# Gate sums moved to the seam, output-gate blocks over five banks, and a sink column, in a hybrid attention block

## The chip, the cores and the metric

The kernel runs on one core of a Trainium2 chip. Its time is the device time of one execution in microseconds (us); the figure of a kernel is the median of several runs. Five engines work side by side and wait for one another by semaphores: PE (matrix products), DVE and POOL (elementwise work), ACT (functions of one argument, copies and casts), and SP, which here only issues DMA transfers. An engine carries out its own instructions strictly in the order in which they stand in its queue.

## The reference

The reference is one decoder layer over 1024 positions of width 1024. All of it is computed in float32.

```python
mod = c @ w_ada[l] + b_ada[l]
shift, scale, gate = jnp.split(mod, 3, axis=-1)
h = rms_norm(x, g_pre[l]) * (1.0 + scale[:, None, :]) + shift[:, None, :]
proj = h @ w_in[l]
q_a, kv_c, kv_s, kv_w, g_nsa, z_a, q_b, kv_b, z_b, merge = jnp.split(proj, pts, axis=-1)
kc = compress_blocks(...)                       # an MLP over overlapping blocks of keys; vc alike
o_a = gts[0] * o_cmp + gts[1] * o_slc + gts[2] * o_win    # compressed, selected, window attention
y_a = (merge_heads(o_a) * jax.nn.silu(z_a)) @ w_o_nsa[l]
o_b = banded_attention(qb, kb, vb, slopes_b, SWA_WINDOW, sinks=sinks[l])
y_b = (merge_heads(o_b) * jax.nn.silu(z_b)) @ w_o_swa[l]
m_a, m_b = jnp.split(merge, 2, axis=-1)
y = (jax.nn.sigmoid(m_a) * y_a + jax.nn.sigmoid(m_b) * y_b) @ w_out[l]
x = x + gate[:, None, :] * rms_norm(y, g_post[l])
```

Two places matter below. The eight 128-row parts of `gate` are needed only by the last line. And the sliding-window attention (`o_b`) has one sink per head, a score that takes part in the softmax's sum and has no value behind it.

## The kernel before

Every float32 product is made of three passes of a matmul over a high and a low part: a weight tile `wraw` is loaded, its high part `wh` is a cast (rounded), and the low part `wl` is the difference, made on POOL (L177). The activations `h` stand in SBUF as `hh` and `hl` in two halves of 512 columns. The three matmuls are L200, L207, L208 in the early blocks, L998, L1003, L1004 in the later ones, L1361 to L1363 in the last part. The sums go to PSUM, whose eight banks are three pools by name: `b_s` (3), `b_pt` (2), `b_pv` (1), `b_pj` (2).

In order of time the kernel does this:

- A prologue (to about 95 us): the norm, the shift and scale, the first projections.
- The z stage (about 95 to 184 us). Six output-gate blocks (ZB0 to ZB3, ZA0, ZA1), each in two halves, are projected into a bank `b_pj`; ACT takes tanh of it (L562), DVE makes the gate (L563) in the tile `sp`, and SP stores that to DRAM (L564). `sp` has one buffer. Between them lie two MLPs that compress keys and values: their first weights come in 16 tiles `w1raw`, cast on ACT (L642), subtracted on DVE (L643), and multiplied on PE (L646 to L648); then come `he` (L650 to L653) and the rest. Beside it POOL makes four input combinations T1 to T4 in eight-way pieces (L731 to L738), which SP stores (L740); DVE makes the gate sums: for each of eight row blocks two products with a reduction over 512 columns (L723), on `w_ada` rows loaded into `wraw`'s buffers. The casts to `wh` in this stage are on DVE (L171), later ones on ACT (L174).
- Units B0 and B1 (184 to about 303 us): sliding-window attention of two key groups. In a task, scores (L856, L859) get the distance added and a running minimum on DVE (L866), exp on ACT (L878), and the sink is added by a subtraction (L884), an exp (L885) and an addition (L886) before the reciprocal (L887).
- Unit A0 (303 to 503 us) and unit A1 (503 to 709 us): the three attentions of the other mixer, one key group each. Between their steps stands a "line" of projection parts that a planner spreads evenly over the unit's PE columns; transfers and casts are hung ahead of a part or behind it. In unit A0 the line holds keys, queries, the blocks ZA2 and ZA3, and the first products of a Strassen-like scheme. In unit A1 it holds products on the sums T2, T1, T3, T4: a set is loaded from DRAM by `set_load` into the place of a half of `h` that is done with (L1049), and formed by `set_form` (cast on ACT, L1056, subtraction on POOL, L1057). Weight sums for the scheme (`paced_sums`, L700 to L706 on POOL) are put at fixed shares of unit A0.
- The seam (709 to 731 us): eight `seam_part`s of 12 matmuls each finish four merge gates; DVE adds their parts (L1345, L1346, L1349), and the heads 4 to 7 of mixer B are loaded (L1311) and split (cast on ACT L1312, subtraction on DVE L1313).
- The gated products of mixer B and then of mixer A (to about 817 us) and the final product (to the end). Beside them DVE and POOL make combinations of the rows of `w_out` (L1411, L1416, and others).

A scheduler orders each engine's queue by the order of the code and by priorities; ties that cost no semaphore ("pace") hold an instruction behind another one in that order.

## Time and profile before

| what | us |
|---|---|
| median of 3 runs | 902.82 (902.55 to 903.59) |
| the profiled execution | 906.57 |
| its span, first to last instruction | 904.7 |
| PE busy in it | 872.4 (96%) |
| DVE / ACT / POOL busy | 659.8 / 530.0 / 537.4 |

The span is the stretch that the trace shows; 1.87 us of the profiled execution lie outside it, and the profiled execution itself is 3.75 us above the median. Mean granted TensorE clock over the span is 0.986 of full speed.

### The profile page before, as it was taken

What the parts mean: (1) busy time and instruction counts of PE and PEld (TensorE: products, weight loads), DVE (VectorE), ACT (ScalarE), POOL (GpSimd) and SP (SyncE); (2) the same over time, 40 slices, a digit from 0 to 9 for tenths busy, and PEclk for the clock granted to TensorE, in tenths of its full rate; (3) what the DMA queues carried; (4) which work ended last, traced back from release to release, by engine and by line L of the source; (5) the groups of instructions that cost most, each with busy time, mean ns of one, the idle gap of its engine ahead of it and who ended that gap; (6) DMA issues with size and microseconds to landing.
All of it is one profiled execution on the core that took longest, in us unless ns stands there. A gap on an engine that the chain in (4) does not pass through costs nothing.

```text
span 904.7 us, 14788 instructions
## 1 busy us (share of the span) xinstructions
PE 872.4 (96%) x4418; PEld 731.0 (81%) x4418; DVE 659.8 (73%) x1637; ACT 530.0 (59%) x1200; POOL 537.4 (59%) x547
## 2 busy tenths in 40 slices
PE   8999988999999989999999999999999999999996
PEld 6989767788888768888888787888888788887885
DVE  4866887648878668666766587776677299788996
ACT  6466631156777777666657697665656375444331
POOL 1001987168786699676446788555666369735551
PEclk8999998999999999999999999999999999999998
DMA  9876566666455456342132533333253399841323
GB/s 352 276 273 206 197 210 223 219 216 208 135 172 156 151 190 185 117 162 72 42 100 72 188 109 120 114 122 124 105 199 128 105 346 303 299 128 59 105 93 117
DMA packets 93297, 151.46 MB, mean 167 GB/s; under 512 B 10913, under 2 KB 28705, under 8 KB 93218
## 3 DMA queue, kind: packets, MB, share of 16 engines
q1 hardware_dynamic: 92064, 149.30, 49.8%
q10 hardware_dynamic: 1154, 1.23, 0.5%
q8 instruction: 35, 0.57, 0.2%
q14 instruction: 44, 0.36, 0.1%
HBM read 108.81 MB, written 38.01 MB: 162 GB/s over the span
## 4 chain that ended last, share of the span: by engine, by line
PE 74%; DMA 3%; DVE 3%; issue 1%; ACT 1%; POOL 0%; DVEq 0%; POOLq 0%; SPq 0%; ACTq 0%
PE b_pt L927 8%; PE b_pj L998 7%; PE b_pj L1003 6%; PE b_pj L1004 6%; PE b_s L859 4%; PE b_pv L938 4%; PE b_s L856 4%; PE b_pv L935 4%; PE b_pj L200 3%; PE b_pj L207 3%; PE b_pj L208 3%; PE b_s L1363 1%; PE b_s L1361 1%; PE b_s L1362 1%; DMA wraw<-in_w_adaT 1%
## 5 line engine op out<-in xcount | busy, mean ns | idle before, releaser
L177 POOL TENSOR_TENSOR wl<-wraw,wh 128x512 fp32r<-128x512 f32 x123 | 170.0, 1386 | 98.8 <-ACT wh L174 80.9
L934 DVE TENSOR_TENSOR pl<-b_pt,ph 128x512 fp32r<-128x512 f32 x162 | 110.6, 686 | 47.4 <-ACT ph L933 46.5
L933 ACT CAST ph<-b_pt 128x512 fp32r<-128x512 f32 x162 | 93.2, 584 | 59.9 <-PE b_pt L927 50.8
L878 ACT ACTIVATE ps<-ps,mins 128x256 f32<-128x256 f32 (+7 forms) x128 | 81.2, 635 | 33.8 <-DVE mins L866 32.9
L174 ACT CAST wh<-wraw 128x512 fp32r<-128x512 f32 x115 | 70.6, 617 | 42.6 <-PE b_pj L1003 18.7
L856 PE MATMUL b_s<-kh,q 128*128 128x256 f32 (+6 forms) x272 | 86.2, 323 | 3.9 <-DVE mins L866 3.0
L200 PE MATMUL b_pj<-hh,wh 128*128 128x512 f32 x208 | 83.7, 403 | 5.2 <-DVE sp L563 5.2
L859 PE MATMUL b_s<-kl,q 128*128 128x256 f32 (+6 forms) x272 | 83.5, 314 | 0.0
L207 PE MATMUL b_pj<-hl,wh 128*128 128x512 f32 x208 | 83.3, 400 | 0.0
L208 PE MATMUL b_pj<-hh,wl 128*128 128x512 f32 x208 | 83.0, 400 | 0.0
L890 POOL TENSOR_SCALAR ps<-ps,rr,gates 128x128 f32<-128x128 f32 (+7 forms) x64 | 52.4, 822 | 50.9 <-DVE rr L882 42.2
L998 PE MATMUL b_pj<-hh,wh 128*128 128x512 f32 x188 | 78.3, 416 | 0.0
L1003 PE MATMUL b_pj<-hl,wh 128*128 128x512 f32 x188 | 74.7, 397 | 0.0
L1004 PE MATMUL b_pj<-hh,wl 128*128 128x512 f32 x188 | 74.4, 396 | 0.0
L938 PE MATMUL b_pv<-pl,V 128*128 128x512 f32 x162 | 68.4, 422 | 1.4 <-DVE pl L934 1.3
L935 PE MATMUL b_pv<-ph,V 128*128 128x512 f32 x162 | 66.6, 411 | 2.7 <-ACT ph L933 1.5
L927 PE MATMUL b_pt<-ident,ps 128*128 128x128 f32 x408 | 67.3, 274 | 0.4 <-DVE pl L934 0.4
L856 PEld LDWEIGHTS b_s<-kh,q 128*128 128x128 f32 x272 | 51.2, 188 | 13.5 <-DVE mins L866 5.2
L890 POOL TENSOR_SCALAR pw<-pw,rr,gates 128x640 f32<-128x640 f32 (+4 forms) x64 | 47.4, 742 | 22.4 <-DVE rr L882 19.6
L927 PEld LDWEIGHTS b_pt<-ident,ps 128*128 128x128 f32 x408 | 51.3, 141 | 10.7 <-DVE pl L934 0.8
L859 PEld LDWEIGHTS b_s<-kl,q 128*128 128x128 f32 x272 | 51.2, 189 | 7.2
L878 ACT ACTIVATE pw<-pw,mins 128x640 f32<-128x640 f32 (+4 forms) x64 | 44.5, 695 | 18.2 <-DVE mins L866 18.0
(454 smaller groups left out, 2474.2 us busy)
## 6 DMA issues: line engine op xcount, KB each, us to landing
wraw<-in_w_blk SPq DMA_DIRECT2D x83, 256.0 KB, 2.9
r<-in_w_out SPq DMA_DIRECT2D x32, 256.0 KB, 4.8
wa<-in_w_adaT SPq DMA_DIRECT2D x15, 512.0 KB, 5.1
wraw<-sS SPq DMA_DIRECT2D x28, 256.0 KB, 2.8
...
```

The lines of the kernel that those rows point to most:

```text
L177: chain("wl", nc.gpsimd.tensor_tensor(wl, raw, wh.bitcast(F32), ALU.subtract))
L200: ins = nc.tensor.matmul(t, lhsT=wh, rhs=hh[kc][half], start=(kc == 0), stop=False)
L207: nc.tensor.matmul(t, lhsT=wh, rhs=hl[kc][half], start=False, stop=False)
L208: nc.tensor.matmul(t, lhsT=wl, rhs=hh[kc][half], start=False, stop=(kc == KC - 1))
L856: ins = nc.tensor.matmul(sp[:, :n_in], lhsT=q, rhs=rh, start=True, stop=False)
L859: nc.tensor.matmul(sp[:, :n_in], lhsT=q, rhs=rl, start=False, stop=True)
L878: nc.scalar.activation(rows[r][:, :off], rows[r][:, :off], AF.Exp, scale=-1.0, bias=last_min[:, r : r + 1], accum_out=sums[:, r : r + 1])
L927: ins = nc.tensor.transpose(t[:, r * P : r * P + P], rows[r][:, off : off + P], ident)
L934: nc.vector.tensor_tensor(pl, t, ph.bitcast(F32), ALU.subtract)
L998: ins = nc.tensor.matmul(self.t, lhsT=wh[:, kc, :], rhs=hi, start=(self.first is None and kc == 0), stop=False)
L1003: nc.tensor.matmul(self.t, lhsT=wh[:, kc, :], rhs=lo, start=False, stop=False)
L1004: ins = nc.tensor.matmul(self.t, lhsT=wl[:, kc, :], rhs=hi, start=False, stop=(kc == KH - 1 and self.stop))
```

## The change

Six things change. The gate sums leave the z stage and are made at the seam, in eight full-width pieces of 1024 columns. The output-gate blocks use `b_s` and `b_pj` by turns, and their tile `sp` has three places: two of three go to the pool `kt` (six buffers). Ten of the twelve `wh` casts of the z stage go from DVE to ACT. The input sums T1 to T4 are tied, in the schedule, to the starts of the output-gate halves (`z_marks`). The sink is written as a 257th column of the score row, so that the one exp with its sum covers it. In unit A0 the output-gate blocks stand last in the line, the T2 and T1 sets are loaded four parts earlier and the first two pieces of T2 formed there, and the weight sums come later; in unit A1 forms are spread one by one.

```diff
     def split_half(raw, shape, low=None):
@@
         if low is None and hold[0] is None and not ended:
-            ins = nc.vector.tensor_copy(wh, raw)
-            after(ins, last["dve"])
+            cast_count[0] += 1
+            if cast_count[0] < 3:
+                after(ins := nc.vector.tensor_copy(wh, raw), last["dve"])
+            else:
+                after(ins := nc.scalar.copy(wh, raw), last["act"])
@@
-        z_out(name, half, proj_half(w, half, lambda: bank("pj")))
+        z_out(name, half, proj_half(w, half, lambda: bank(("s", "pj")[z_count[0] % 2])))
@@
-        sp = kq.tile([P, HS], F32, name="sp", tag="sp", bufs=1)
+        z_count[0] += 1
+        if hold[0] is None and z_count[0] % 3:
+            sp = kq.tile([P, HS], F32, name="sp", tag="kt", bufs=6)
+        else:
+            sp = kq.tile([P, HS], F32, name="sp", tag="sp", bufs=1)
@@
-    for k in range(8):
-        gate_sum(k)
-    nc.vector.tensor_tensor(amod, mod[:, 16:24], g_post, ALU.mult)
@@
-                    row = whole_row[:, 256 * r : 256 * r + 256]
+                    if r == 0:
+                        sink = 128 * min(i, 1) + 128
+                        nc.scalar.copy(whole_row.rearrange("p (r c) -> p r c", r=4)[:, :, sink],
+                                       nsink[:, 4 * g : 4 * g + 4])
+                    row = whole_row[:, 257 * r : 257 * r + 257]
@@
-            nc.vector.tensor_tensor(rr, last_min, nsink[:, 4 * g : 4 * g + 4], ALU.subtract)
-            nc.scalar.activation(rr, rr, AF.Exp)
-            nc.vector.tensor_tensor(sums, sums, rr, ALU.add)
@@
-                line += raw_products([2, 3]) + plan_z("A", 2) + raw_products([4]) + plan_z("A", 3)
-                line += plan_k(1, 0) + plan_q("A", 1, 0) + raw_products([5, 6])
+                line += raw_products([2, 3, 4]) + plan_k(1, 0) + plan_q("A", 1, 0) + raw_products([5, 6])
+                za, zb = plan_z("A", 2), plan_z("A", 3)
+                line += za[:2] + zb[:2] + za[2:] + zb[2:]
@@
-                behind(line[-1], half_free)
+                behind(line[-5], half_free)
+                for k in range(2):
+                    ahead_of(line[k - 2], lambda k=k: set_form("T2", (k,)))
@@
-                    for f, share in zip(paced_sums(p), (0.02, 0.07)):
-                        pieces.append((begun + whole[u] * (share + 0.14 * n), lambda at, f=f: f()))
+                    for f, share in zip(paced_sums(p), (0.18, 0.23)):
+                        paced(share + 0.09 * n, f)
@@
+        gate_c = op.tile([P, S], F32, name="cg", tag="oh0")
+        places = ["oh1", "oh2", "oh3", "ol0", "ol1"]
+        def gate_load(k):
+            wa = op.tile([P, S], F32, name="wg", tag=places[k % 5])
+            nc.sync.dma_start(wa, io["w_adaT"][(16 + k) * P : (17 + k) * P, :])
+            owing.append((16 + k, wa))
+        def gate_sum():
+            blk, wa = owing.pop(0)
+            nc.vector.tensor_tensor_reduce(
+                out=wa, in0=wa, in1=gate_c, scale=1.0, scalar=smalls[:, 8 + blk : 9 + blk],
+                op0=ALU.mult, op1=ALU.add, accum_out=mod[:, blk : blk + 1])
```

At the seam the transfer of `c` and two `gate_load`s stand in each of the four rounds behind the loads of that round, and two `gate_sum`s in each round but the first; the last two follow the loop.

The first place is DVE's queue in the z stage, from the fourth low part of the first MLP's weights on. `w1` are these weights, `wh` are casts, `he` is the MLP's hidden tile, `gpart` a half gate sum, `sp` the output gates. Before:

```order
L643 TENSOR_TENSOR w1_1195<-w1raw_1192,w1_1194 128x512
L643 TENSOR_TENSOR w1_1207<-w1raw_1204,w1_1206 128x512
L635 TENSOR_TENSOR fl_1176<-flat_1168,fh_1175 128x2048
L171 CAST wh_1591<-wraw_1587 128x512
L643 TENSOR_TENSOR w1_1219<-w1raw_1216,w1_1218 128x512
L651 TENSOR_SCALAR he_1146<-he_1146 126x256
L171 CAST wh_1595<-wraw_1589 128x512
L652 RECIPROCAL he_1146<-he_1146 126x256
L563 SCALAR_TENSOR_TENSOR sp_1441<-sp_1441,b_pj_1416 128x512
L653 TENSOR_TENSOR he_1146<-b_pt_1049,he_1146 126x256
L723 ISA wraw_1799,gpart_1730<-wraw_1799,cg_1731,smalls_79 128x512
L723 ISA gpart_1730 128x1
```

After:

```order
L654 TENSOR_TENSOR w1_1195<-w1raw_1192,w1_1194 128x512
L654 TENSOR_TENSOR w1_1207<-w1raw_1204,w1_1206 128x512
L646 TENSOR_TENSOR fl_1176<-flat_1168,fh_1175 128x2048
L654 TENSOR_TENSOR w1_1219<-w1raw_1216,w1_1218 128x512
L662 TENSOR_SCALAR he_1146<-he_1146 126x256
L663 RECIPROCAL he_1146<-he_1146 126x256
L574 SCALAR_TENSOR_TENSOR sp_1441<-sp_1441,b_pj_1416 128x512
L664 TENSOR_TENSOR he_1146<-b_pt_1049,he_1146 126x256
L574 SCALAR_TENSOR_TENSOR sp_1483<-sp_1483,b_s_1457 128x512
L669 COPY h1T_1154<-b_pt_1151 128x252
L574 SCALAR_TENSOR_TENSOR sp_1512<-sp_1512,b_pj_1487 128x512
```

The casts and the half sums are gone from DVE's queue between the MLP's steps, and the blocks' `sp` come from `b_s` and `b_pj` by turns.

The second place is the seam, from the last merge gates on. On DVE, `t2` are the merge gates, `wg` the gate sums, `r` rows of `w_out`, `ol7` the low part of the last head of mixer B, which the gated products need. Before:

```order
L1346 TENSOR_TENSOR t2_8789<-t2_8789,b_pt_8798 128x512
L1313 TENSOR_TENSOR ol6_8677<-t1_8678,oh6_8676 128x512
L1349 TENSOR_TENSOR t2_8789<-t2_8789,b_s_8820 128x512
L1345 TENSOR_TENSOR t2_8835<-t2_8835,b_pj_8845 128x512
L1313 TENSOR_TENSOR ol6_8677<-t1_8682,oh6_8676 128x512
L1346 TENSOR_TENSOR t2_8836<-t2_8836,b_pj_8845 128x512
L1411 TENSOR_TENSOR r_8919<-r_8919,r_8918 128x512
L1349 TENSOR_TENSOR t2_8836<-t2_8836,b_s_8867 128x512
L1416 TENSOR_TENSOR r_8922<-r_8923,r_8919 128x512
L1411 TENSOR_TENSOR r_9023<-r_9023,r_9022 128x512
L1313 TENSOR_TENSOR ol7_8687<-t1_8688,oh7_8686 128x512
L1313 TENSOR_TENSOR ol7_8687<-t1_8692,oh7_8686 128x512
```

After:

```order
L1359 ISA wg_8718,mod_83<-wg_8718,cg_8610,smalls_79 128x1024
L1359 ISA mod_83 128x1
L1378 TENSOR_TENSOR t2_8767<-t2_8767,b_pj_8781 128x512
L1379 TENSOR_TENSOR t2_8768<-t2_8768,b_pj_8781 128x512
L1359 ISA wg_8720,mod_83<-wg_8720,cg_8610,smalls_79 128x1024
L1359 ISA mod_83 128x1
L1384 TENSOR_TENSOR t2_8768<-t2_8768,b_s_8804 128x512
L1451 TENSOR_TENSOR r_8860<-r_8860,r_8859 128x512
L1359 ISA wg_8771,mod_83<-wg_8771,cg_8610,smalls_79 128x1024
L1359 ISA mod_83 128x1
L1327 TENSOR_TENSOR ol7_8601<-t1_8602,oh7_8600 128x512
L1327 TENSOR_TENSOR ol7_8601<-t1_8606,oh7_8600 128x512
```

Seven gate sums stand before the two `ol7` instructions now (four of them further up), and two of the three operations on `r` stand behind them. On SP, in the same place, `od7` is that head, `w_o` the weights of the gated products, the first of which here belongs to the fourth block. Before:

```order
L1389 DMA r_8923<-in_w_out 128x512
L1389 DMA r_9022<-in_w_out 128x512
L1389 DMA r_9023<-in_w_out 128x512
L1389 DMA r_9026<-in_w_out 128x512
L1311 DMA t1_8688<-od7_125 128x512
L164 DMA wraw_9039<-in_w_o 128x512
L1311 DMA t1_8692<-od7_125 128x512
L164 DMA wraw_9092<-in_w_o 128x512
L164 DMA wraw_9149<-in_w_o 128x512
```

After:

```order
L1354 DMA wg_8720<-in_w_adaT 128x1024
L1429 DMA r_8859<-in_w_out 128x512
L1429 DMA r_8860<-in_w_out 128x512
L1354 DMA wg_8771<-in_w_adaT 128x1024
L1325 DMA t1_8602<-od7_125 128x512
L1429 DMA r_8863<-in_w_out 128x512
L1325 DMA t1_8606<-od7_125 128x512
L1429 DMA r_8864<-in_w_out 128x512
L1429 DMA r_8963<-in_w_out 128x512
L1325 DMA t1_8912<-od0_118 128x512
L1429 DMA r_8964<-in_w_out 128x512
L1429 DMA r_8967<-in_w_out 128x512
L164 DMA wraw_8980<-in_w_o 128x512
L164 DMA wraw_9033<-in_w_o 128x512
```

From the first load of the seam (`od4`) up to that `w_o`, 23 transfers of 256 KB were asked for before (5.75 MB); now these are 25, with `c` and seven `wg` of 512 KB beside them (10.25 MB). On PE the first matmul on `ol7` is the 50th of the gated products before and the 58th after.

The third place is ACT's queue where unit A0 ends and unit A1 begins. `hht` are the forms of the T1 and T2 sets from `hlt`, `ph` are the casts of transposed attention rows, which the next matmul in PE's queue waits for. Before:

```order
L933 CAST ph_5863<-b_pt_5858 128x512
L933 CAST ph_5874<-b_pt_5869 128x512
L1056 CAST hht0_6032<-hlt0_6033 128x512
L933 CAST ph_5892<-b_pt_5887 128x512
L1056 CAST hht1_6035<-hlt1_6036 128x512
L174 CAST wh_6239<-wraw_6237 128x512
L1100 COPY acc_5965<-b_pj_5930 128x512
L1056 CAST hht2_6038<-hlt2_6039 128x512
L933 CAST ph_5913<-b_pt_5908 128x512
L1056 CAST hht3_6041<-hlt3_6042 128x512
L933 CAST ph_5924<-b_pt_5919 128x512
```

After:

```order
L1062 CAST hht0_5743<-hlt0_5744 128x512
L939 CAST ph_5520<-b_pt_5515 128x512
L1062 CAST hht1_5746<-hlt1_5747 128x512
L1062 CAST hht2_5749<-hlt2_5750 128x512
L911 CAST ph_5645<-b_pt_5642 128x256
L887 ACTIVATE ps_5616,sums_5546<-ps_5616,mins_5548 128x1024
L1062 CAST hht3_5752<-hlt3_5753 128x512
L1062 CAST hht4_5731<-hlt4_5732 128x512
L573 ACTIVATE sp_5727<-b_pj_5609 128x512
L1062 CAST hht5_5734<-hlt5_5735 128x512
```

The forms still stand between the casts `ph`, and the whole of the set is formed some instructions earlier; the transfers into `hlt` are asked for behind an earlier part of the line (`line[-5]` for `line[-1]`).

## Rows read from the trace of the kernel before

**Rows 1.** The page of the kernel before, the chain that ended last: shares of the span by engine.

```profile
PE 74%; DMA 3%; DVE 3%; issue 1%; ACT 1%; POOL 0%; DVEq 0%; POOLq 0%; SPq 0%; ACTq 0%
```

**Rows 2.** Busy time of each engine in 20-us stretches: PE, PEld, DVE, ACT, POOL, then granted clock, DMA share, GB/s.

```profile
100.00:120.00 20.00, 17.90 (x89) 14.97 (x88) 18.87 (x18) 7.74 (x11) 19.35 (x12) 0.91 0.57 185
120.00:140.00 20.00, 15.06 (x70) 12.38 (x69) 14.87 (x12) 5.90 (x9) 17.58 (x12) 0.87 0.70 234
...
320.00:340.00 20.00, 18.00 (x95) 14.61 (x96) 12.92 (x72) 14.03 (x46) 20.00 (x29) 1.00 0.55 187
...
720.00:740.00 20.00, 20.00 (x90) 16.57 (x89) 15.70 (x22) 15.65 (x27) 9.07 (x7) 1.00 1.02 371
740.00:760.00 20.00, 20.00 (x90) 16.56 (x89) 20.00 (x20) 11.20 (x21) 20.00 (x13) 1.00 0.83 268
```

**Rows 3.** What PE's instructions waited for over the whole span: the waiting line, what ended the wait; us in total, times, the longest.

```profile
PE b_pj L200 <- DVE sp L563: 5.2, 2, 4.9
PE b_s L856 <- DVE mins L866: 3.0, 5, 0.9
PE b_pt L646 <- ACT w L642: 2.1, 1, 2.1
PE b_pt L656 <- DVE he L653: 1.9, 1, 1.9
...
PE b_pv L935 <- ACT ph L933: 1.5, 1, 1.5
...
PE b_pv L935 <- DVE ot L952: 1.1, 1, 1.1
```

**Rows 4.** PE's timeline at the longest of these waits: start, duration, in brackets the idle time before.

```profile
137.55 0.79 PE L200 MATMUL b_pj<-hh,wh 128*128 128x512 f32 x1 [4.94 <-DVE sp L563]
138.14 0.63 PE L207 MATMUL b_pj<-hl,wh 128*128 128x512 f32 x1
138.56 0.63 PE L208 MATMUL b_pj<-hh,wl 128*128 128x512 f32 x1
...
141.54 0.39 PE L200 MATMUL b_pj<-hh,wh 128*128 128x512 f32 x1
141.77 0.39 PE L207 MATMUL b_pj<-hl,wh 128*128 128x512 f32 x1
```

**Rows 5.** What the engines waited for between 85 and 185 us (columns as in rows 3).

```profile
ACT sp L562 <- DMA sp_ZB<-sp: 32.4, 6, 9.9
...
PE b_pt L647 <- DVE w L643: 0.9, 2, 0.7
```

**Rows 6.** DVE's groups between 95 and 185 us: shape, count, busy us, mean ns, idle before.

```profile
L723 DVE CUSTOM_DVE_ANT_0 wraw<-wraw,cg,smalls 128x512 f32<-128x512 f32 x8 | 6.9, 867 | 5.0 <-DMA wraw<-in_w_adaT 4.8
...
L171 DVE CAST wh<-wraw 128x512 fp32r<-128x512 f32 x9 | 6.4, 722 | 2.8 <-PE b_pj L207 2.0 <-DMA wraw<-in_w_blk 0.9
...
L723 DVE CUSTOM_DVE_ANT_0 wraw<-wraw,cg,gpart 128x512 f32<-128x512 f32 x8 | 6.5, 814 | 3.0 <-DMA wraw<-in_w_adaT 2.8
```

**Rows 7.** DVE's timeline in the same stage (columns as in rows 4).

```profile
113.54 6.24 DVE L643 TENSOR_TENSOR w<-w1raw,w 128x512 fp32r<-128x512 f32 x4
...
136.87 0.62 DVE L563 SCALAR_TENSOR_TENSOR sp<-sp,b_pj 128x512 f32<-128x512 f32 x1
```

**Rows 8.** PE's timeline where unit A0 ends.

```profile
502.45 0.51 PE L935 MATMUL b_pv<-ph,V 128*128 128x512 f32 x1 [1.55 <-ACT ph L933]
...
505.79 0.63 PE L998 MATMUL b_pj<-hh,wh 128*128 128x512 f32 x1
...
506.92 0.39 PE L935 MATMUL b_pv<-ph,V 128*128 128x512 f32 x1
```

**Rows 9.** ACT's timeline at the same time.

```profile
501.29 0.62 ACT L1056 CAST hht<-hlt 128x512 fp32r<-128x512 f32 x1 [3.62 <-DMA hlt<-T1d]
```

**Rows 10.** DVE's timeline in unit B0, at a task's first score row.

```profile
197.07 0.48 DVE L866 CUSTOM_DVE_ANT_0 ps<-b_s,tab,nsink 128x256 f32<-128x256 f32 x1 [1.55 <-POOL ps L704]
```

**Rows 11.** DVE's groups over the whole span (columns as in rows 6): a sum of the same shape as the seam's (L285), the heads' low parts, two operations on rows of w_out, and the sink's subtraction.

```profile
L285 DVE CUSTOM_DVE_ANT_0 wa<-wa,cb,smalls 128x1024 f32<-128x1024 f32 x15 | 18.7, 1279 | 0.9 <-DMA wa<-in_w_adaT 0.9
L1313 DVE TENSOR_TENSOR ol<-t,oh 128x512 fp32r<-128x512 f32 x16 | 18.1, 1145 | 9.9 <-ACT oh L1312 9.9
...
L1411 DVE TENSOR_TENSOR r<-r 128x512 f32<-128x512 f32 x4 | 6.0, 1504 | 0.0
...
L1416 DVE TENSOR_TENSOR r<-r 128x512 f32<-128x512 f32 x4 | 5.3, 1330 | 0.0
...
L884 DVE TENSOR_TENSOR rr<-mins,nsink 128x4 f32<-128x4 f32 x16 | 15.6, 974 | 0.2
```

**Rows 12.** DVE's timeline in the seam.

```profile
722.78 1.34 DVE L1313 TENSOR_TENSOR ol<-t,oh 128x512 fp32r<-128x512 f32 x2 [8.39 <-ACT oh L1312]
...
738.73 5.10 DVE L1313 TENSOR_TENSOR ol<-t,oh 128x512 fp32r<-128x512 f32 x3 [1.26 <-ACT oh L1312]
```

**Rows 13.** PE's timeline at the start of the gated products of mixer B, and at the first use of the last head's low part.

```profile
730.78 0.39 PE L1361 MATMUL b_pt<-oh,wh 128*128 128x512 f32 x1
...
741.89 0.39 PE L1362 MATMUL b_pt<-ol,wh 128*128 128x512 f32 x1
```

**Rows 14.** Busy time in 4-us stretches of the seam (columns as in rows 2).

```profile
720.00:724.00 4.00, 4.00 (x20) 3.30 (x19) 1.22 (x2) 2.06 (x4) 1.29 (x1) 1.00 0.92 270
...
732.00:736.00 4.00, 4.00 (x20) 3.30 (x19) 4.00 (x7) 3.34 (x7) 2.49 (x2) 1.00 1.05 405
```

More of the change, by code (lines that the diff above doesn't have):

```diff
@@ L693, in hybrid_kernel @@
             mlp(1)
+        z_marks = []
         for _ in zs:
-            pass
+            z_marks.append(last["pj"])
     def pair_sums(p, a11, a12, a21, a22):
@@ L710, in spare @@
         return [kq.tile([P, HS], F32R, name="q", tag="q", bufs=8) for _ in range(n)]
-    gate_c, gate_part = [], sm.tile([P, 8], F32, name="gpart")
-    for h in range(2):
-        gate_c.append(kq.tile([P, HS], F32, name="cg", tag="kt", bufs=6))
-        nc.sync.dma_start(gate_c[h], io["c"][h * HS : h * HS + HS].partition_broadcast(P))
-    def gate_sum(k):
-        blk, part = 16 + k, gate_part[:, k : k + 1]
-        for h in range(2):
-            wa = wp.tile([P, HS], F32, name="wraw", tag="wraw", bufs=3)
-            nc.sync.dma_start(wa, io["w_adaT"][blk * P : blk * P + P, h * HS : h * HS + HS])
-            nc.vector.tensor_tensor_reduce(
-                out=wa, in0=wa, in1=gate_c[h], scale=1.0, scalar=part if h else smalls[:, 8 + blk : 9 + blk],
-                op0=ALU.mult, op1=ALU.add, accum_out=mod[:, blk : blk + 1] if h else part)
     def input_sums(k):
@@ L730, in input_sums, with at_mark, store @@
         b11, b21, b12, b22 = (t.bitcast(F32) for t in spare(4))
[L731 to L740 removed]
+        def at_mark(n, ins):
+            n += 3 * k
+            if n < len(z_marks):
+                after(ins, z_marks[n])
+        def store(n, name, t):
+            at_mark(n, nc.sync.dma_start(t_dram[name][k], t))
+        at_mark(0, nc.sync.dma_start(b12, h_dram[k]))
+        at_mark(0, nc.sync.dma_start(b22, h_dram[k + 4]))
+        for t, kk in ((b11, k), (b21, k + 4)):
+            at_mark(0, op_(t, hh[kk][0].bitcast(F32), hl[kk][0].bitcast(F32), ALU.add))
+        at_mark(1, op_(b22, b22, b12, ALU.subtract))
+        at_mark(1, op_(b12, b12, b11, ALU.subtract))
+        at_mark(1, op_(b11, b22, b11, ALU.add))
+        store(2, "T3", b22)
+        store(2, "T1", b12)
+        at_mark(2, op_(b21, b21, b11, ALU.subtract))
+        store(2, "T2", b11)
+        store(3, "T4", b21)
     for k in range(KH):
         input_sums(k)
[L744 to L746 removed]
     at = attn_es.enter_context(tc.tile_pool(name="at", bufs=1, reuse_waits="tile"))
@@ L877, in scores @@
                 rows.append(row)
+            on = off + (br == "swa")
             nc.scalar.activation(
[L879 removed]
+                rows[r][:, :on], rows[r][:, :on], AF.Exp, scale=-1.0, bias=last_min[:, r : r + 1],
                 accum_out=sums[:, r : r + 1])
@@ L1244, in hybrid_kernel @@
                 for k in range(KH):
-                    ahead_of(line[11 + k], lambda k=k: set_form("T3", (k,)))
+                    ahead_of(line[11 + 2 * k], lambda k=k: set_form("T3", (k,)))
                 e = [last_products(p) for p in range(NP - 4)]
-                line += [e[0][0], e[1][0], e[0][1], e[1][1]] + e[2]
-                ahead_of(e[1][0], lambda: set_form("T4", range(KH)))
+                line += [e[0][0], e[1][0], e[2][0], e[0][1], e[1][1], e[2][1]]
+                for f, ks in ((e[1][0], (0,)), (e[2][0], (1,)), (e[0][1], (2, 3))):
+                    ahead_of(f, lambda ks=ks: set_form("T4", ks))
             for n, f in enumerate(line):
@@ L1350, in hybrid_kernel @@
             nc.scalar.activation(y, y, AF.Sigmoid)
+            if n:
+                gate_sum()
             early[b, 1], early[b, 0] = e, y
+        while owing:
+            gate_sum()
+        nc.vector.tensor_tensor(amod, mod[:, 16:24], g_post, ALU.mult)
         def gated(m, c, side, emit):
```

27 lines of the change are left out of this document (14 added, 13 removed).

## The prediction

> **What bounds the kernel now.** I read the chain of waits first: PE holds 74% of it [rows 1], so time is lost where PE stands still or runs slowly. The 20-us stretches show where: 2.1 us idle at 100 to 120, 4.9 at 120 to 140, 2.0 at 320 to 340, nothing at 720 to 760 [rows 2]. The list of PE's waits names the causes [rows 3]; the timelines give the rest.
>
> In the z stage four lines wait: 5.2 us for the output-gate block's DVE step, 2.1 for an MLP weight's cast, 1.9 for the hidden tile, 0.9 for weights' low parts [rows 3, 5], 10.1 in all. Behind the 4.94-us wait the matmuls stand 0.42 us apart (138.14 to 138.56) until 141.5, and 0.23 apart from there [rows 4]; that is TensorE's lower level, 1.2 instead of 2.4 GHz, for some 3.9 us and costs about 1.9. The granted clock is 0.91 at 100 to 120 [rows 2], so half speed for about 3.6 of 20 us; taking three of them as worked, about 1.6 us more. Together 13.6 us are there to be had.
>
> The cause is the spill. ACT waited six times, 32.4 us, for the store of the single `sp` buffer [rows 5]; a bank comes free only after tanh and the DVE step, so two `b_pj` banks and one `sp` hold PE. DVE is also full there: 18.87 of 20 us at 100 to 120 [rows 2].
>
> **The z stage after.** Removed from DVE: 16 half gate sums, 6.9 + 6.5 us, and most of the nine casts, 0.72 each [rows 6]. Ten casts go to ACT, which was busy 7.74 and 5.90 of 20 us [rows 2] and stood waiting for the store, so I take them as hidden; if that cover is gone, a cast costs ACT about 0.6 (the form at 501.29 took 0.62, [rows 9]) and shows at PE only when it is late. Removed from SP's queue: 16 transfers of 256 KB, behind which spill stores stood. Three spill buffers and five banks take away the store's wait, so the whole 5.2 us, the clock loss behind it, and most of the 2.1 go. Next in line are the MLP's own steps on DVE: four low parts take 6.24 us, 1.56 each [rows 7], while PE works on one weight tile for six matmuls of 256 columns, by half of 0.23 us each 0.7 us. A group of four is then 4 x (1.56 - 0.7) = 3.4 us late where PE stands before it with nothing else, and the hidden tile's chain, 1.9, keeps its length. 13.6 - 3.4 - 1.9 = 8.3 us gained. Bounds: 4 (the waits of the list only move to the MLP) and 12.
>
> **Unit A0.** POOL is busy 20.00 of 20 us at 320 to 340 and PE idles 2.0 [rows 2], mostly for the running minimum on DVE, 3.0 us over five waits [rows 3]. The weight sums, POOL work, are moved from shares 0.02 and 0.07 to 0.18 and 0.23, so POOL is freer at the start, but the same work comes at 0.09 instead of 0.14 of the unit apart. I take +1, bounds -2 and +3.
>
> **The end of unit A0.** PE waits 1.55 us for a cast at 502.45, then runs with 0.63-us matmuls at 505.79 and 0.39 at 506.92 [rows 8], about 1.3 us lost to the lower clock; about 2.9 together. The cast stood on ACT behind a form that waited 3.62 us for its transfer from T1 [rows 9]. The loads now stand four parts earlier in a line of some 34 parts over 200 us, some 20 us, but ACT's forms are earlier too and stand close behind them, so part of the wait may stay. +1.5, bounds 0 and 2.9. The later forms of T3, one each second part: PE waited 1.1 us for DVE's `ot` there [rows 3]; +0.3, bounds -1 and +1.4.
>
> **The sink.** Per task three instructions go (the subtraction 0.97 us on DVE [rows 11] among them) and one ACT copy comes. PE has no wait in the list of that stage that names them, so their removal gains nothing. The copy writes the row before the scores: it waits for the row's buffer on ACT, where before DVE waited, once 1.55 us, for POOL's pair sums [rows 10]. 0, bounds -1.5 and +1.
>
> **The seam.** Eight sums of 1024 columns at 1.279 us [rows 11] are new there, with 4 MB of weights and `c`. DVE was idle 8.39 us before 722.78, but then only 1.26 before 738.73 [rows 12], and busy 20.00 of 20 at 740 to 760 [rows 2]. In DVE's order the first gate sum follows the first merge gates, so the earlier idle time is of little use. Seven sums before the last head's low part are 7 x 1.28 = 9.0; of that 1.26 fit into the idle time and 1.50 + 1.33 go behind it with two row operations [rows 11]: 4.9 us later. The first of its two instructions ended about 738.73 + 1.70 = 740.4 [rows 12], so now 745.3. PE came to it at 741.89, in the 50th of the gated matmuls that began at 730.78 [rows 13]; as the 58th that is 8 x 0.227 later, 743.7. PE waits 1.6 us and, as at 502, may lose some 1.4 to the clock behind it.
>
> The queue of transfers: 5.75 MB stood up to the fourth block's weights, now 10.25. At 405 GB/s (732 to 736, [rows 14]) 4.5 MB are 11 us. From 720, with 270 GB/s up to 724 [rows 14], 10.25 MB (some 0.6 of them landed before) have landed at about 745 to 746; cast and POOL's subtraction, behind other work there, bring the low part to 749 to 751, and by the order PE comes to it as the 81st of the gated matmuls, at 730.78 + 80 x 0.227 = 748.9, or 1.6 later with the wait above. I take 1.0 us for that. Seam: -1.6 - 1.4 - 1.0 = -4.0; bounds -1 and -12.
>
> The row that bears on this price is the 405 GB/s. The Trainium skill, "DMA: Bandwidth & Descriptors", section "Where 436 GB/s comes from", gives about 358 GB/s per core for transfers between HBM and SBUF and 435 for the fabric. This case's 405 lies above the first, so I go by the row; by 358 the added 4.5 MB would be 12.6 us and the sum 1.5 worse.
>
> **The sum.** 8.3 + 1 + 1.5 + 0.3 + 0 - 4.0 = 7.1 us. The profiled execution was 906.57, of which 899.5 would be left. It lay 3.75 above the median of the runs, 902.82; taken from the median, 895.7.
>
> **The rivals.**
>
> A: the z stage's stalls only move. Once the spill is free, PE is held by the MLP's chain. For it: the 1.56 us per low part, double what PE needs, and the casts, now on ACT, ahead of the MLP's. Against it: PE's list gives the MLP lines only 4.9 of 10.1 us. Then the z stage gives 4: 4 + 2.8 - 4 = 2.8, so 900.0.
>
> B: the seam is ruled by DVE, and the kernel is slower. Price: a gate sum takes not 1.28 but some 1.7 times that, as the heads' low parts do (1.145 mean against 0.67 in the pair at 722.78 [rows 11, 12]). Then 7 x 2.17 = 15.2, less 4.1, is 11.1 us late; PE had 1.46 us of slack (740.43 to 741.89) and gets 1.8 by its order, so waits 7.8, loses 1.4 to the clock, and the later rows and heads, behind DVE busy without a gap to 760 [rows 2], add 4 more: 13. It decides from 11.1 us on, where it takes all that the rest gains; with a z stage of only 6 the sum is 6 + 2.8 - 13 = -4, so 907. For it: DVE has no idle time from 740 to 760. Against: POOL is busy only 9.07 of 20 us at 720 to 740 [rows 2], where the sums stand, and the slow rows are those beside a busy POOL.
>
> For this there is a page. The Trainium skill, "VectorE: DVE Perf Modes", section "Two Vector instructions with no wait between them", has the second SBUF read interface shared with GpSimd, which a product of two SBUF tensors needs. By that rule the sums would slow beside POOL. The trace agrees where POOL is nearly full (19.35 of 20 us at 100 to 120), 1.56 us for a low part; it doesn't show a gate sum there.
>
> C: everything is had. The gate sums fill gaps at the seam (cost 1), the z stage gives 11: 11 + 2.8 - 1 = 12.8, so 890. For it: ACT and DVE had room enough in the second half of the stage. Against: DVE's queue is in order.
>
> **How the numbers follow.** The forecast 0.48, A 0.17, B 0.20, C 0.15. The forecast's own range is 892 to 899. The range 888 to 907 takes in C's bulk, A, and most of B; the ends of all bounds together (883 and 912) are left out. A measurement of this kernel can't tell less than about 0.2%, 1.8 us. Faster by more than that (below 901.0): the forecast nearly whole, C, and two thirds of A, 0.73. Within: 0.08, from A and from the mild end of B. Slower: 0.19, the rest of B.
>
> **What would show it.** In the changed profile, the z stage's list should no longer have PE waiting for the blocks' DVE step, nor ACT for the spill's store; granted clock at 120 to 140 should be near 0.95 or above; the stage should end about 8 us sooner. The wait at the end of A0 should be below 1 us. In the seam a wait of 1 to 3 us on DVE's `ol` near the start of the gated products should be new, and gate sums should take 1.3 us. Wrong would be: MLP waits of 8 us or more in the z stage (A), gate sums near 2 us and PE idle 8 us or more between 730 and 780 (B), no wait there at all (C).

## The result and the profile after

The changed kernel takes 894.62 us (median of 4 runs, 891.47 to 895.18), the kernel before 903.21 in the same runs: ratio 0.989, 95% interval 0.9857 to 0.9924, so 7 to 13 us faster. 895.7 was forecast. Its profiled execution took 895.18 us, where 899.5 was forecast; that of the kernel before lay 3.4 us above its median, so the two profiles lie 11.4 us apart and the medians 8.6.

The table cuts both traces at the same matmuls (start of the first MLP matmul, of the first score of unit A0 and of A1, of the first seam matmul, of the first and last gated product).

| stretch, us | before | after | gain | forecast |
|---|---|---|---|---|
| start to the first MLP matmul | 103.4 | 103.4 | 0.0 | 0 |
| first MLP matmul to A0 | 193.5 | 181.4 | 12.1 | 8.3 |
| A0 | 202.3 | 200.5 | 1.8 | 1 |
| A1 | 209.6 | 205.5 | 4.1 | 1.8 |
| seam | 22.1 | 22.1 | 0.0 | |
| gated products | 88.0 | 94.8 | -6.9 | -4.0 (seam and this) |

PE's busy time in the second stretch, before and after (columns as in [rows 2]):

```profile
103.37:296.87 193.50, 183.41 (x944) 153.02 (x943) 147.14 (x316) 101.82 (x254) 136.07 (x139) 0.97 0.60 193
103.41:284.80 181.39, 178.46 (x946) 150.87 (x944) 112.78 (x252) 107.52 (x267) 134.25 (x142) 1.00 0.56 180
```

PE idles 10.1 us in it before and 2.9 after.

From the page of the changed kernel, what answers to [rows 1]:

```profile
PE 82%; DMA 5%; DVE 4%; issue 3%; ACT 2%; POOL 2%; SPq 1%; DVEq 0%; POOLq 0%; ACTq 0%
```

Busy time in 20-us stretches, as [rows 2] (PE, PEld, DVE, ACT, POOL, granted clock, DMA share, GB/s):

```profile
100.00:120.00 20.00, 17.78 (x97) 14.54 (x96) 16.41 (x14) 10.99 (x16) 18.77 (x13) 1.00 0.52 168
120.00:140.00 20.00, 20.00 (x102) 16.93 (x101) 11.50 (x15) 9.06 (x14) 11.89 (x11) 1.00 0.75 254
...
320.00:340.00 20.00, 20.00 (x114) 17.11 (x113) 14.85 (x63) 15.15 (x40) 19.61 (x24) 1.00 0.69 204
700.00:720.00 20.00, 20.00 (x90) 16.57 (x89) 14.13 (x23) 9.32 (x14) 3.82 (x3) 1.00 0.98 362
720.00:740.00 20.00, 16.46 (x58) 12.23 (x57) 19.39 (x24) 9.11 (x16) 12.12 (x8) 0.83 0.97 361
```

At 120 to 140 PE is busy throughout at full clock, where it had 15.06 of 20 us at 0.87. At 720 to 740, full before, it now has 16.46 at a clock of 0.83. What PE waited for, as [rows 3]:

```profile
PE b_pt L658 <- DVE w L654: 2.6, 4, 0.7
PE b_pt L1401 <- ACT oh L1326: 1.8, 1, 1.8
...
PE b_s L864 <- DVE mins L874: 1.7, 1, 1.7
...
PE b_pt L1401 <- ACT wh L179: 1.1, 1, 1.1
...
PE b_pt L1402 <- DVE ol L1327: 0.6, 1, 0.6
```

The block's DVE step, first in the old list, is gone, and with it the cast, the hidden tile and most of the wait at the end of A0 (0.55 left). The z stage keeps 2.6 us for low parts of MLP weights (L658 <- L654), four waits of 0.7 at most. Three waits in the gated products are new (L1401, L1402), and one wait of 1.7 for the running minimum stands where five of 0.9 at most stood before.

PE's timeline there:

```profile
727.05 0.50 PE L1401 MATMUL b_pt<-oh,wh 128*128 128x512 f32 x1 [1.83 <-ACT oh L1326]
...
728.78 0.80 PE L1402 MATMUL b_pt<-ol,wh 128*128 128x512 f32 x1 [0.59 <-DVE ol L1327]
729.37 0.63 PE L1403 MATMUL b_pt<-oh,wl 128*128 128x512 f32 x1
729.80 0.63 PE L1402 MATMUL b_s<-ol,wh 128*128 128x512 f32 x1
...
735.67 0.40 PE L1402 MATMUL b_s<-ol,wh 128*128 128x512 f32 x1
737.18 0.50 PE L1401 MATMUL b_pt<-oh,wh 128*128 128x512 f32 x1 [1.12 <-ACT wh L179]
```

PE stands 1.83, 0.59 and 1.12 us; behind the first two the matmuls are 0.43 us apart until 734.5, and then 0.23, so the lower clock again. The three waits are 3.5 us, and 5.7 us at half the rate cost about 2.9, together 6.4 of the 6.9.

The first of them is for the cast of the last head's first half, `oh`. What stood around it, on ACT, on SP (which asks for the transfers) and on DVE:

```profile
725.86 0.62 ACT L1423 CAST hhw<-r 128x512 fp32r<-128x512 f32 x1 [0.46 <-DVE r L1451]
726.39 0.61 ACT L1326 CAST oh<-t 128x512 fp32r<-128x512 f32 x1
727.25 0.62 ACT L1326 CAST oh<-t 128x512 fp32r<-128x512 f32 x1 [0.24 <-DMA t<-od]
...
735.99 0.62 ACT L1423 CAST hhw<-r 128x512 fp32r<-128x512 f32 x1 [2.72 <-DVE r L1451]
736.52 1.13 ACT L179 CAST wh<-wraw 128x512 fp32r<-128x512 f32 x2
```

```profile
717.92 0.33 SPq L1325 DMA_DIRECT2D t<-od  x1
719.11 0.33 SPq L1429 DMA_DIRECT2D r<-in_w_out  x1
719.78 0.33 SPq L1325 DMA_DIRECT2D t<-od  x1
```

```profile
722.85 1.28 DVE L1359 CUSTOM_DVE_ANT_0 wg<-wg,cg,smalls 128x1024 f32<-128x1024 f32 x1
...
724.65 1.18 DVE L1451 TENSOR_TENSOR r<-r 128x512 f32<-128x512 f32 x1
725.75 1.27 DVE L1359 CUSTOM_DVE_ANT_0 wg<-wg,cg,smalls 128x1024 f32<-128x1024 f32 x1
...
727.03 3.38 DVE L1327 TENSOR_TENSOR ol<-t,oh 128x512 fp32r<-128x512 f32 x2
```

The cast at 726.39 stands on ACT behind a cast of `w_out` rows (725.86), which waits for DVE's L1451 (724.65), which stands behind the gate sum of 722.85. So a gate sum on DVE can hold PE by way of ACT's queue, two steps off. But the head itself was late. Its second half was cast as soon as it had landed (727.25). Its first half, asked for at 717.92, landed at 725.99 (the last update of its semaphore in the trace). Without the queue on ACT the cast could have begun 0.40 us earlier and no more, so of PE's 1.83 us about 1.4 belong to the transfer and 0.4 to ACT's queue. The low part began at 727.03, when the cast and the last of seven gate sums ended together, and its halves took 1.69 us each: that is the 0.59. The third wait, 1.12, is for the fifth block's weights; they had landed at 731.68, and their cast (736.52) stood behind a row cast that waited 2.72 us for DVE.

### The profile page after: what moved, and what is told of

It is laid out like the page before. It is cut to its first block, busy times and chain, and to the rows that moved or that the text cites. A ratio compares the mean times of both kernels' runs of the same rounds, so it can differ in the third digit from the quotient of the medians.

```text
span 893.3 us, 14739 instructions
## 1 busy us (share of the span) xinstructions
PE 868.8 (97%) x4418; PEld 730.1 (82%) x4418; DVE 630.2 (71%) x1579; ACT 534.1 (60%) x1210; POOL 532.7 (60%) x547
## 4 chain that ended last, share of the span: by engine, by line
PE 82%; DMA 5%; DVE 4%; issue 3%; ACT 2%; POOL 2%; SPq 1%; DVEq 0%; POOLq 0%; ACTq 0%
PE b_pt L933 7%; PE b_pj L1004 6%; PE b_pj L1010 6%; PE b_pj L1009 6%; PE b_pv L944 4%; PE b_s L867 4%; PE b_pj L212 4%; PE b_pj L213 4%; PE b_pj L205 4%; PE b_s L864 4%; PE b_pv L941 4%; DMA wg<-in_w_adaT 2%; PE b_s L228 1%; PE b_s L229 1%; DVE w L654 1%
## 5 line engine op out<-in xcount | busy, mean ns | idle before, releaser
L182 POOL TENSOR_TENSOR wl<-wraw,wh 128x512 fp32r<-128x512 f32 x123 | 167.0, 1361 | 80.7 <-ACT wh L179 61.4
L887 ACT ACTIVATE ps<-ps,mins 128x257 f32<-128x257 f32 (+9 forms) x128 | 81.3, 636 | 34.8 <-DVE mins L874 32.4
L1004 PE MATMUL b_pj<-hh,wh 128*128 128x512 f32 x188 | 77.7, 413 | 0.0
L1010 PE MATMUL b_pj<-hh,wl 128*128 128x512 f32 x188 | 74.5, 396 | 0.0
L1009 PE MATMUL b_pj<-hl,wh 128*128 128x512 f32 x188 | 74.0, 393 | 0.0
L205 PE MATMUL b_pj<-hh,wh 128*128 128x512 f32 x160 | 63.1, 394 | 0.0
L213 PE MATMUL b_pj<-hh,wl 128*128 128x512 f32 x160 | 63.0, 394 | 0.0
L212 PE MATMUL b_pj<-hl,wh 128*128 128x512 f32 x160 | 62.9, 393 | 0.0
```

What stands on the lines that cost most here:

```text
L182: chain("wl", nc.gpsimd.tensor_tensor(wl, raw, wh.bitcast(F32), ALU.subtract))
L887: nc.scalar.activation(rows[r][:, :on], rows[r][:, :on], AF.Exp, scale=-1.0, bias=last_min[:, r : r + 1], accum_out=sums[:, r : r + 1])
L1004: ins = nc.tensor.matmul(self.t, lhsT=wh[:, kc, :], rhs=hi, start=(self.first is None and kc == 0), stop=False)
L1009: nc.tensor.matmul(self.t, lhsT=wh[:, kc, :], rhs=lo, start=False, stop=False)
L1010: ins = nc.tensor.matmul(self.t, lhsT=wl[:, kc, :], rhs=hi, start=False, stop=(kc == KH - 1 and self.stop))
```

## The experiments

All times are medians beside the kernel before on the same chip; the stretches are cut as above, from the profiled execution of each (one per kernel). The rows come from four batches, in which the kernel before lay at 903.2 to 904.2.

| kernel | MLP to A0 | A0 | A1 | seam | gated | time | ratio to before (95%) |
|---|---|---|---|---|---|---|---|
| before | 193.5 | 202.3 | 209.6 | 22.1 | 88.0 | 903.2 to 904.2 | |
| after | 181.4 | 200.5 | 205.5 | 22.1 | 94.8 | 894.6 | 0.989 (0.9857 to 0.9924) |
| loads_only | 180.5 | 199.2 | 205.6 | 22.1 | 96.5 | 894.0 | 0.9877 (0.9842 to 0.9911) |
| sums_only | 180.9 | 198.2 | 205.3 | 22.1 | 98.2 | 894.6 | 0.9892 (0.9854 to 0.993) |
| sums_in_A1 | 180.4 | 199.3 | 209.2 | 23.2 | 87.5 | 889.8 | 0.9834 (0.9802 to 0.9866) |
| sums_behind_A1 | 180.7 | 202.6 | 205.0 | 31.1 | 90.0 | 895.9 | 0.9897 (0.9877 to 0.9918) |
| sums_tied_A1 | 181.4 | 199.5 | 207.2 | 22.1 | 89.2 | 889.8 | 0.9846 (0.9805 to 0.9888) |
| before_seam | 188.2 | 200.8 | 209.2 | 22.0 | 95.3 | 906.7 | 1.0027 (0.9996 to 1.0059) |
| one_spill | 184.8 | 197.7 | 205.1 | 22.1 | 94.2 | 894.3 | 0.9889 (0.9866 to 0.9913) |
| two_banks | 184.5 | 201.2 | 205.5 | 22.1 | 92.8 | 894.4 | 0.9888 (0.9846 to 0.993) |
| casts_dve | 183.6 | 201.3 | 205.9 | 22.1 | 95.4 | 895.2 | 0.9901 (0.987 to 0.9931) |
| no_tie | 180.5 | 201.1 | 205.0 | 22.1 | 94.0 | 893.4 | 0.9879 (0.9836 to 0.9922) |
| old_lines | 180.9 | 197.8 | 207.7 | 22.1 | 93.9 | 891.8 | 0.9867 (0.9846 to 0.9887) |
| no_sink_col | 178.8 | 201.3 | 204.9 | 22.1 | 94.3 | 893.0 | 0.987 (0.9848 to 0.9893) |

**The seam: loads without sums.**

```diff
-                out=wa, in0=wa, in1=gate_c, scale=1.0, ...
+                out=wa[:, :8], in0=wa[:, :8], in1=gate_c[:, :8], scale=1.0, ...
```

> The changed kernel with the seam's loads kept and each gate sum cut to 8 of its 1024 columns, so that DVE does almost none of that work (the gate sums are left out of the result). Theory 1: the 6.9 us that the gated products of mixer B and A take longer (94.8 us from the first to the last of them against 88.0 before) come from the seven sums of 1.28 us in DVE's queue ahead of the row operation and of the last head's low part. Then these waits go, the stretch is 88 to 89 us and the time 888 +- 1. Theory 2: they come from the 4.5 MB of added transfers, which make the last head and the fourth block's weights land late. Then 2 to 4 us of waits and the lower clock behind them stay, the stretch is 92 to 95 us and the time 892 to 895.

The gated products take 96.5 us, more than either theory's range. PE's timeline:

```profile
723.04 0.50 PE L1401 MATMUL b_pt<-oh,wh 128*128 128x512 f32 x1 [1.35 <-ACT oh L1326]
...
724.29 0.50 PE L1402 MATMUL b_pt<-ol,wh 128*128 128x512 f32 x1 [0.29 <-DVE ol L1327]
...
731.83 0.80 PE L1401 MATMUL b_pj<-oh,wh 128*128 128x512 f32 x1 [3.85 <-ACT wh L179]
```

The last wait, 3.85 us, is for the fourth block's weights, which PE did not wait for in the changed kernel. ACT's timeline leads back from it:

```profile
722.37 0.62 ACT L1326 CAST oh<-t 128x512 fp32r<-128x512 f32 x1 [0.47 <-DMA t<-od]
...
727.67 0.62 ACT L1423 CAST hhw<-r 128x512 fp32r<-128x512 f32 x1 [2.10 <-DVE r L1456]
730.63 0.62 ACT L1423 CAST hhw<-r 128x512 fp32r<-128x512 f32 x1 [2.35 <-DVE r L1451]
731.16 0.61 ACT L179 CAST wh<-wraw 128x512 fp32r<-128x512 f32 x1
```

The weights had landed at 728.68. Their cast (731.16) stands behind row casts that wait for DVE, 2.10 and 2.35 us; DVE works without a gap from 723.02, where it had waited for the last head; and the head's cast (722.37) waited for its transfer, asked for at 715.01 and landed 7.3 us later. So with the sums nearly gone the late transfers bring the same loss, through the same queues. Theory 1 alone falls.

**The seam: sums without loads.**

```diff
-            wa = op.tile([P, S], F32, name="wg", tag=places[k % 5])
-            nc.sync.dma_start(wa, ...)
+            if k == 0:
+                wa = op.tile(...); nc.sync.dma_start(wa, ...)
+            else:
+                wa = first_wg[0]
```

> The changed kernel with all eight full gate sums on DVE, but only the first block of rows (and c) loaded, so 3.5 MB of the seam's transfers are left out (and with them the result's gate). Theory 1 (DVE's queue): the stretch of the gated products stays at 93 to 95 us and the time at 893 to 895. Theory 2 (transfers): 88 to 89 us, 888 +- 1.

98.2 us, above the 93 to 95 of Theory 1: the loss stands without the transfers as well. DVE's timeline:

```profile
724.47 2.32 DVE L1363 CUSTOM_DVE_ANT_0 wg<-wg,cg,smalls 128x1024 f32<-128x1024 f32 x1
...
728.41 2.31 DVE L1363 CUSTOM_DVE_ANT_0 wg<-wg,cg,smalls 128x1024 f32<-128x1024 f32 x1
...
732.33 1.75 DVE L1327 TENSOR_TENSOR ol<-t,oh 128x512 fp32r<-128x512 f32 x1
```

The last three sums of this kernel stand beside a POOL that is busy throughout 720 to 737 (two of them 5 to 6 us later behind the start of the seam than in the changed one), and there they took 2.3 us each; PE waited 2.58 us for a low part. So this run shows that sums on DVE alone can hold PE as long; it doesn't give DVE's share in the changed kernel, as their places differ. Neither theory is enough: left in alone, each in an order of its own, the transfers cost all of it, and so do the sums.

**Both elsewhere.** In sums_in_A1 loads and sums leave the seam and stand at the end of unit A1:

```diff
+    gate_c = at.tile([P, S + 4], F32, name="cg", tag="ps", bufs=4)[:, :S]
+    nc.sync.dma_start(gate_c, io["c"].partition_broadcast(P))
+    for blk in range(16, 24):
+        wa = at.tile([P, S + 4], F32, name="wg", tag="ps", bufs=4)[:, :S]
+        nc.sync.dma_start(wa, io["w_adaT"][blk * P : blk * P + P, :])
+        nc.vector.tensor_tensor_reduce(out=wa, in0=wa, in1=gate_c, ...)
```

> The changed kernel with the eight gate sums, loads and all, not at the seam but at the end of unit A1, in the score rows' buffers that are free by then; DVE is busy 6.5 of 20 us and transfers run at 73 GB/s there. Theory 1 and 2 alike: the seam is as before, the gated products take 88 us, the time is 887 to 889, faster than either kernel. Rival: the loads (4.5 MB, 11 us at 400 GB/s) stand in the queue before the seam's own and bring the first heads late, or the sums hold up the attention's last steps on DVE; then 892 or more.

The gated products are back at 87.5 us and the time is 889.8, below both kernels: 4.8 us below the changed one, 13.7 below the one before. It misses the 887 to 889 forecast, since unit A1 is 3.7 us longer and the seam 1.1. DVE and PE in A1:

```profile
682.72 1.28 DVE L1313 CUSTOM_DVE_ANT_0 wg<-wg,cg,smalls 128x1024 f32<-128x1024 f32 x1 [1.40 <-DMA wg<-in_w_adaT]
...
683.93 0.69 DVE L940 TENSOR_TENSOR pl<-b_pt,ph 128x512 fp32r<-128x512 f32 x1
```

```profile
684.67 0.72 PE L944 MATMUL b_pv<-pl,V 128*128 128x512 f32 x1 [2.05 <-DVE pl L940]
```

The first sum waits for its transfer, the low part `pl` stands behind it, and PE waits 2.05 us for that. Two tries to mend it:

```diff
 sums_behind_A1: every sum tied behind the last step of the attention on DVE
-        nc.vector.tensor_tensor_reduce(...)
+        after(nc.vector.tensor_tensor_reduce(...), lows[0])
 sums_tied_A1: each sum tied behind one of the last five low parts
+        after(nc.vector.tensor_tensor_reduce(...), lows[min(blk - 21, -1)])
```

> As sums_in_A1 (gate sums at the end of unit A1), but tied behind the last attention step on DVE (ot), so that no sum that waits for its transfer stands ahead of a low part (pl) that PE needs. If the 2.05-us wait at 684.67 in sums_in_A1 (and 0.67 behind it) came from that order, both go, unit A1 is 3 to 4 us shorter and the time 885 to 887. If not (the transfers on SP's queue then hold the seam's loads), the seam has new waits and the time is 889 or more.

The wait in A1 went (205.0), and the seam took 31.1 us: the other case. SP's queue, what its loads of `wg` waited for (columns as in [rows 3]), and PE:

```profile
704.48 3.03 SPq L1312 DMA_DIRECT2D wg<-in_w_adaT  x2
...
711.40 1.38 SPq L1334 DMA_DIRECT2D t<-od  x3
```

```profile
SPq L1312 <- DVE mod L1313: 4.0, 2, 2.2
```

```profile
721.09 0.76 PE L1384 MATMUL b_pt<-oh,wh 128*128 128x512 f32 x1 [8.85 <-DVE sgm L1369]
```

Loads that wait for a sum's buffer stand in SP's queue ahead of the heads' (711.40, 11.6 us later than the same load at 699.76 in the changed kernel). On DVE the heads' low parts stand ahead of the addition (L1369) that PE waits 8.85 us for.

> As sums_in_A1, with the first sum tied behind the low part (pl) that stood behind it there, and each further sum behind one low part more. In sums_in_A1 the first sum waited 1.40 us for its transfer with that low part behind it, and PE 2.05 us; that wait and the lower clock after it should go: unit A1 206 to 207 us instead of 209.2, time 886 to 888. Rival: as in sums_behind_A1 the loads, which wait on SP's queue for the buffer of a sum, then hold the seam's loads (there od4 was asked for 17 us after the last pl, and PE waited 8.85 us); then the seam has a wait of 2 us or more and the time is 890 or above.

A1 takes 207.2 and the wait of 2.05 is gone, three of 0.6 to 0.9 us and two of 0.5 to 0.65 in the gated products came. The span is 886.4 against 886.8 and the time the same, 889.8: the wait was given back in small pieces, and the 886 to 888 expected wasn't reached.

**The gate sums' share of the z stage.** before_seam is the kernel before with the gate sums alone moved, by the same lines as the change.

> The kernel before with one thing changed: the gate sums go from the z stage to the seam, as in the changed kernel. Theory 1: the z stage was held by the single spill buffer, so with it unchanged the wait for the block's DVE step stays (3 us or more of it) and the stage is less than 4 us shorter; the seam costs its 6.9 us, time 905 to 909. Rival: the stage was held by DVE's load and SP's queue (16 loads, 13.4 us of sums); then it is 8 us or more shorter and the time 899 to 902.

The MLP stretch is 5.3 us shorter, the gated products 7.3 longer, the time the same or slightly longer (906.7; the interval holds 1). PE still waits 1.80 us for the block's DVE step at 134.43 and 2.22 for the cast at 113.56. So Theory 1 holds in the time (905 to 909), not in the share: the gate sums were nearly half of what the z stage lost.

**The rest of the z stage, one part undone at a time:**

```diff
 one_spill:
-        if hold[0] is None and z_count[0] % 3:
+        if False:
 two_banks:
-        ... bank(("s", "pj")[z_count[0] % 2])
+        ... bank("pj")
 casts_dve:
-            if cast_count[0] < 3:
+            if cast_count[0] < 99:
 no_tie:
-                after(ins, z_marks[n])
+            pass
```

> The changed kernel with the output gates' tile back to its single buffer; all else stays. Theory 1 (the spill store's wait holds the blocks): the wait of PE for the block's DVE step comes back, 3 to 6 us of it with the lower clock, unit A0 begins at 288 to 291 instead of 284.8, time 898 to 901. Rival: with the gate sums gone from DVE and SP one buffer is enough; then less than 1.5 us, 894 to 896.

> The changed kernel with the output-gate blocks in the two b_pj banks alone, three places for sp kept. Theory 1: the store was what held a bank; without its wait two banks do, A0 begins at 282 to 285.5 and the time is 893 to 896. Rival: the banks are what counts, since ACT and DVE reach a block late when they work on the MLP; then PE waits 2 us or more for the block's DVE step, A0 begins at 287 or later and the time is 897 to 901.

> The changed kernel with all twelve casts of the z stage on DVE, as before. Six profiles with the changed z stage show unit A0 beginning at 281.8 to 284.8 us. Theory 1 (DVE's load holds the MLP's steps): with 7 us of casts back between them PE waits 2 us or more longer for low parts or the hidden tile, A0 begins at 286 or later, the time is 896 to 899. Rival: with the gate sums gone DVE has room; A0 begins below 285.5 and the time is 893 to 896.

> The changed kernel without the ties of the input sums T1 to T4 to the block starts. Theory 1: POOL's order hardly matters for PE there; A0 begins at 281.5 to 286, time 893 to 896. Rival: untied, the sums (1.3 to 1.7 us each on POOL) stand ahead of low parts of weights that PE needs; then A0 begins at 287 or later and the time is 897 or more.

The MLP stretch takes 184.8, 184.5 and 183.6 us where the first three are undone, against 180.4 to 181.4 in the seven profiles that have this stage and units B0 and B1 as changed: 3.9, 3.7 and 2.7 more than their mean of 180.9. With one buffer ACT waits for the store again, and less than before (32.4 us over six waits, [rows 5]):

```profile
ACT sp L573 <- DMA sp_ZB<-sp: 17.6, 4, 9.6
```

A0 begins at 286.3, 286.5 and 286.9 us, later than in the changed kernel, but the time doesn't follow: 894.3 to 895.2 can't be told from 894.6 with intervals of 4 to 8 us. PE idles 5.3, 3.9 and 4.8 us in the stretch, against 2.2 to 3.0 in those seven; with two banks the rest is other matmuls, which stand in the stretch there. In none of the three does PE wait for the block's DVE step, and the granted clock stays at 1.00: PE waits a little longer for the MLP's low parts (4.3 us with one buffer, 2.6 in the changed kernel). So the parts are shown in single profiles alone, at 1 to 3 us of PE's idle time each. The wait that Theory 1 of one_spill and the rival of two_banks had come back stays away, and none of the three is its cause by itself. The ties do nothing (180.5).

**The lines of A0 and A1, and the sink.** old_lines has the code of units A0 and A1 from the kernel before; no_sink_col adds the sink as before.

```diff
 old_lines: the two lists, set_load, set_form and paced_sums as in the kernel before
 no_sink_col:
+            nc.vector.tensor_tensor(rr, last_min, nsink[:, 4 * g : 4 * g + 4], ALU.subtract)
+            nc.scalar.activation(rr, rr, AF.Exp)
+            nc.vector.tensor_tensor(sums, sums, rr, ALU.add)
```

> The changed kernel with the lines, loads and forms of units A0 and A1 as before. From the start of unit A0 to the seam the kernel before took 411.9 us, the changed one 405.9. Theory 1: the lines make this difference (POOL's weight sums at the start of A0, the loads at its end); then 410.5 to 412.5 us and a time of 898 to 901. Rival: it comes from the shorter row of waits elsewhere; then below 408 and 894 to 896.

The stretch is 405.5 us, as with the new lines (402.8 to 407.2 in those eight profiles with the gate sums at the seam): Theory 1 falls. The new lines do shorten A1, 205.3 on the mean of these eight (204.9 to 205.9) against 207.7. A0 takes 200.1 on the same mean against 197.8, but the eight reach from 197.7 to 201.3. Where A0 loses, in the changed kernel:

```profile
389.33 1.30 POOL L712 TENSOR_TENSOR sb<-sb 128x512 f32<-128x512 f32 x1 [7.17 <-DMA sb<-in_w_blk]
```

```profile
398.60 2.21 DVE L543 CAST kh<-kc 128x64 fp32r<-128x64 f32 x1 [3.23 <-POOL sa L718]
```

```profile
401.26 0.44 PE L864 MATMUL b_s<-kh,q 128*128 128x384 f32 x1 [1.65 <-DVE mins L874]
```

A weight sum, moved later, waits 7.17 us on POOL for its transfer; DVE's copy of keys waits 3.23 for the end of that sum; PE waits 1.65 for the running minimum behind the copy. Waits for the running minimum come to 0 to 3.5 us in the profiles with the new lines: where they are 0.2 or less (loads_only, sums_only, one_spill) A0 takes 197.7 to 199.2, as with the old lines, and in the others 199.3 to 202.6. With the old lines none is longer than 0.9. What makes the transfer late isn't shown.

> The changed kernel with the sink added as before by a subtraction, an exp and an addition per task. Theory 1: the sink hides beside PE in units B0 and B1; the time from the start of unit A0 and the whole stay within 1.5 us, 893 to 896. Rival: the shorter chain on DVE (24 us of busy time less) is part of the gain; then unit A0 begins 2 us or more later and the time is 897 or more.

893.0 us, the same within the interval. A0 begins earlier and takes longer; from the first MLP matmul to the seam it is 585.0 us, between loads_only (585.3) and sums_only (584.4), whose code up to there is the changed kernel's. Within what these runs can tell, the sink is worth nothing either way, as forecast.

## Why the prediction was right, and which steps were not

The time was right to 1.1 us; the profiled execution was 4.3 us better than the sum. Gains and losses were both larger than their terms, and the part that outgrew the sum is about what the profile of before lay above its median, so the agreement is closer than the terms were, and in part luck. One of the prediction's sums is wrong: its lower bounds add up to 12.5 us, which is 915 and not 912; nothing else hangs on it.

- **z stage, +8.3 forecast, 12.1 measured (in a stretch that holds units B0 and B1 too).** Which waits go was right, as was the next in line: four low parts, 2.6 us, forecast 3.4. Mis-sized was the hidden tile's chain, taken as staying at 1.9: PE waits for it no more in the changed kernel. Waits and lower clock together give 13.6 - 2.9 = 10.7. Of the other 1.4 us, about one is work: five projection matmuls of 0.23 us fewer stand in the stretch after (557 and 552); the rest isn't placed. The cause was named too narrowly. "The cause is the spill" fails: moving the gate sums alone gave 5.3 us (before_seam), and the single buffer costs only 3.9 when it is put back, without the wait for the block's DVE step.
- **A0, +1 forecast, 1.8 measured, for another reason.** The step "POOL is freer at the start" because the weight sums come later failed: with the old lines A0 takes 197.8, no longer than the shortest with the new ones. That A0 gains with the old lines too has its cause upstream; POOL waited 3.3 us for a weight sum's transfer early in A0 before, and not in old_lines, but what made the transfer late isn't shown. The later sums brought the wait at 401 in the changed kernel.
- **The end of A0, +1.5 and +0.3 forecast, 4.1 measured in A1.** The wait went (0.55 left at 477, full clock), by new lines 2.4 us of A1. The rest of A1's gain came with the other parts, since the old lines have it too (207.7 against 209.6, and a granted clock of 1.00 where A1 had 0.99 before); which of them isn't shown. The forecast took all from the lines.
- **Sink, 0:** right.
- **Seam, -4.0 forecast, -6.9 measured.** The stretch was right, and that a wait near the first use of the last head would be new. The path was not. The 1.6 us were put on DVE's queue ahead of the low part, but the head itself landed late (725.99) and its cast came 0.40 later still, behind a row operation on ACT that waited for DVE: 1.83 us, and 0.59 for the low part. The queue of transfers was reckoned for the fourth block's weights alone and not for the head. The 1.0 us put on those weights agrees with the 1.12 by luck: PE didn't wait for the fourth block's, and the fifth block's, landed 4.8 us before their cast, waited on ACT. The clock term, 1.4, measured about 2.9: it was taken from one wait, and here a second wait follows the first.
- **Rival B's price** of a slow gate sum beside POOL shows in sums_only (2.31 us against 1.28), but the changed kernel's first seven stood where POOL was idle all or most of the time and took 1.28, as argued; only the eighth took 2.02.

The Trainium skill's "DMA: Bandwidth & Descriptors", section "Where 436 GB/s comes from", has about 358 GB/s as the limit between HBM and SBUF, and in the same note 425 for a 16 MB measurement; the seam ran at 362 over 700 to 720 with its start-up in it, and at 400 to 417 in each 4 us from 710 to 734, so the measurement decides for the higher rate.
